# GpSimd's low parts of the mixer weights: a negated copy on ACT and an accumulating DMA in place of a subtraction

## The chip, the core and the metric

The kernel runs on one core of a Trainium2 chip (trn2). The core has five engines that work side by side, each through its own instructions in order: TensorE (PE, the matmuls; PEld are its weight loads), VectorE (DVE), ScalarE (ACT), GpSimd (POOL) and SyncE (SP, which issues most DMAs). ACT and POOL issue DMAs too. They wait for one another through semaphores. The metric is the time of one execution on the device in microseconds (us); lower is better.

## The reference

A bidirectional encoder of two layers over 512 tokens of 1024 channels, all in float32. A layer is a half-weighted SwiGLU block, a mixer, and another half-weighted SwiGLU block:

```python
for l in range(DEPTH):                       # DEPTH = 2
    x = x + 0.5 * swiglu(rmsnorm(x, ffn1_norm[l]), ...)      # 1024 -> 2816 -> 1024
    h = rmsnorm(x, mix_norm[l]); p = h @ w_in[l]             # 1024 -> 2048
    a, f, q, k, v = split(p)                                 # 256, 256, 512, 512, 512
    y_pool = pool_mixer(a, pool_w[l], pool_scale[l])         # window means minus token, a map, a scale
    y_four = fourier_mixer(f, fourier_w[l])                  # real part of a 2-D DFT, a map
    y_attn = diff_attention(q, k, v, lam, ...)               # 4 heads, softmax minus lam * softmax
    x = x + concat(y_pool, y_four, y_attn) @ w_out[l]        # 1024 -> 1024
    x = x + 0.5 * swiglu(rmsnorm(x, ffn2_norm[l]), ...)
return rmsnorm(x, final_norm)
```

## The kernel before

Channels lie on the 128 partitions and tokens along a row, so `x` is eight tiles of 128x512. TensorE multiplies in a faster float32 form that keeps fewer bits (`F32R`). To keep the accuracy, every operand is split into a high part `hi`, rounded to that form, and a low part `lo = x - hi`; a product is then three matmuls (`mm3`): high by high (L107), high by low (L108), low by high (L109).

**Weights.** They arrive in pieces of 128x1024 (512 KB), or 128x768, on SP's queue (L158), each in a staging tile `st`, of which there are seven. Some pieces of the SwiGLU blocks have a second piece added by an accumulating DMA that POOL issues (L160, L175), since these blocks use a scheme with fewer multiplications on sums of weights. `split` makes the operand of a piece: ACT copies `st` into `hi` (L103), then VectorE or GpSimd writes `lo = st - hi` (L104). There are four `hi` and four `lo` tiles, handed out in turn; a new one is written when the matmuls of the operand four places before it are done. `produce` runs three operands ahead of the matmuls (AHEAD), and loads five pieces ahead (RAWS).

**The mixer.** A mixer has twelve groups of weights of two pieces each, so 24 operands: P0 to P3 (queries and keys of a head), V0 and V1 (values), A (pooling group), F (Fourier group), and W0a, W1a, W2, W3 (the output projection). P1, P2, V1 and W3 stand in the table `ON_VECTOR`, and their low parts are written by VectorE. Those of the other eight, 16 operands in a mixer and 32 in all, are written by GpSimd.

The steps of a mixer are emitted in the order of the table `ORDER`, and a scheduler then places each engine's instructions. The steps that matter here, in that order: N is the norm of the mixer's input; P0 to P3 project; E0 to E3 split a head's queries and keys (`qs`, `kh`, `kl`: copies on ACT, differences on DVE); S is the scores of a head and a block of queries (DVE adds the bias and finds the maximum, ACT takes the exponential, one of three engines scales, DVE joins both softmaxes at L574, all in tiles `sc`); T transposes the scores on PE (`th`, `tl` are their parts); VE scales the values (`vh`, `vl`); X multiplies scores by values (`AV`, then `osq`, `osh`, `osl` for the head's norm); Y ends the head (`t`, `yo`, `yh`, `yl`); AE makes the window sums of the pooling group (`pad`, `win`, `m`), PL0 and PL1 multiply them by the pooling map (`PL`; the parts of `m` are tiles `g`); GH, FE, FG, FD are the Fourier group; W0a to W3 multiply by the output projection.

What sets an order there: each engine is in order, so a copy on ACT that waits holds up what stands behind it, and the same on POOL, whose queue also holds the sums of squares for the norms (L282), scalings of scores (L573), low parts of head outputs (`yl`, `osl`) and the issues of accumulating DMAs.

## Time and profile before

| | us |
|---|---|
| three runs | 1862.51, 1863.81, 1864.34 (median 1863.81) |
| profiled execution, its time | 1862.69 |
| profiled execution, its span | 1860.9 |
| mixer of the first layer, about | 374 to 565 |
| mixer of the second layer, about | 1285 to 1476 |
| POOL busy in the span | 307.2 |
| of it the 32 subtractions of weight pieces | 82.1 |

The span runs from the first instruction to the end of the last one of the profiled execution; 1.8 us of its time lie around it. A row of a timeline reads: start, length (both in us), engine, line of the kernel, operation, what it writes and reads, and in brackets how long the engine was idle before it and what ended that. "PE L109" is the matmul of line 109. Rows that group instructions give the busy time and the mean length in ns of one, and behind the bar the idle time of the engine ahead of them with what ended most of it. The lines that the argument needs are shown in the prediction.

### The profile page before, as it was taken

What the parts mean: (1) busy time and instruction counts of PE and PEld (TensorE: products, weight loads), DVE (VectorE), ACT (ScalarE), POOL (GpSimd) and SP (SyncE); (2) the same over time, 40 slices, a digit from 0 to 9 for tenths busy, and PEclk for the clock granted to TensorE, in tenths of its full rate; (3) what the DMA queues carried; (4) which work ended last, traced back from release to release, by engine and by line L of the source; (5) the groups of instructions that cost most, each with busy time, mean ns of one, the idle gap of its engine ahead of it and who ended that gap; (6) DMA issues with size and microseconds to landing.
All of it is one profiled execution on the core that took longest, in us unless ns stands there. A gap on an engine that the chain in (4) does not pass through costs nothing.

```text
span 1860.9 us, 28011 instructions
## 1 busy us (share of the span) xinstructions
PE 1773.0 (95%) x11249; PEld 1604.4 (86%) x11249; DVE 1355.0 (73%) x1962; ACT 853.6 (46%) x1193; POOL 307.2 (17%) x272
## 2 busy tenths in 40 slices
PE   7899999999798999999989999999987989999997
PEld 7889989877577989989889899898776888899896
DVE  6865856889779774856898477478978896568474
ACT  6433524457446433524554244243864554244243
POOL 1101101223313101101130010103232220010101
PEclk9899999999899999999999999999998999999998
DMA  8666857433215757857578586664221366586561
GB/s 250 146 168 150 199 131 170 136 94 91 71 35 125 175 154 158 202 139 164 155 156 205 125 204 159 141 167 137 69 80 49 83 149 181 128 186 181 130 165 46
DMA packets 76738, 262.91 MB, mean 141 GB/s; under 512 B 8640, under 2 KB 11712, under 8 KB 76608
## 3 DMA queue, kind: packets, MB, share of 16 engines
q0 software_dynamic: 24768, 90.19, 28.5%
q1 hardware_dynamic: 48672, 167.26, 27.7%
q10 hardware_dynamic: 3168, 3.68, 0.7%
q8 instruction: 88, 1.44, 0.3%
q14 instruction: 42, 0.34, 0.1%
HBM read 258.99 MB, written 2.10 MB: 140 GB/s over the span
## 4 chain that ended last, share of the span: by engine, by line
PE 78%; DVE 11%; ACT 4%; DMA 3%; issue 3%; POOL 0%; DVEq 0%; ACTq 0%; SPq 0%; POOLq 0%
PE dn L107 8%; PE dn L108 7%; PE dn L109 7%; PE qg L414 4%; PE qg L415 4%; PE qg L416 4%; PE qe L414 4%; PE qe L415 4%; PE qe L416 4%; PE qa L416 4%; PE qa L415 4%; PE qa L414 4%; DMA st<-in_gu 3%; DVE lo L104 2%; PE qb L415 2%
## 5 line engine op out<-in xcount | busy, mean ns | idle before, releaser
L103 ACT ACTIVATE hi<-st 128x1024 fp32r<-128x1024 f32 (+2 forms) x452 | 466.5, 1037 | 668.2 <-PE dn L108 216.7
L104 DVE TENSOR_TENSOR lo<-st,hi 128x1024 fp32r<-128x1024 f32 (+2 forms) x420 | 505.4, 1206 | 179.2 <-ACT hi L103 178.2
L108 PE MATMUL dn<-al,hi 128*128 128x512 f32 x704 | 274.6, 390 | 0.0
L109 PE MATMUL dn<-ah,lo 128*128 128x512 f32 x704 | 274.0, 389 | 0.0
L107 PE MATMUL dn<-ah,hi 128*128 128x512 f32 x704 | 271.9, 392 | 0.6
L175 POOL DMA_DIRECT2D st<-in_gu x129 | 116.0, 903 | 656.7 <-DVE lo L104 546.7
L414 PE MATMUL qg<-xh,hi 128*128 128x256 f32 x688 | 197.4, 287 | 9.0 <-DVE w L432 7.9
L415 PE MATMUL qg<-xh,lo 128*128 128x256 f32 x688 | 196.7, 286 | 0.0
L416 PE MATMUL qg<-xl,hi 128*128 128x256 f32 x688 | 196.7, 286 | 0.0
L414 PE MATMUL qe<-xh,hi 128*128 128x256 f32 x608 | 173.3, 285 | 14.6 <-ACT xh L103 8.4
L512 DVE SCALAR_TENSOR_TENSOR x<-dn,x 128x512 f32<-128x512 f32 x96 | 66.1, 688 | 164.7 <-PE dn L109 164.7
L415 PE MATMUL qe<-xh,lo 128*128 128x256 f32 x608 | 172.5, 284 | 2.1 <-DVE lo L104 2.1
L416 PE MATMUL qe<-xl,hi 128*128 128x256 f32 x608 | 172.4, 283 | 1.8 <-DVE xl L104 1.8
L107 PEld LDWEIGHTS dn<-ah,hi 128*128 128x128 f32 x704 | 131.3, 188 | 32.5 <-ACT ah L103 6.5
L108 PEld LDWEIGHTS dn<-al,hi 128*128 128x128 f32 x704 | 132.2, 188 | 28.9 <-DVE al L104 2.4
L109 PEld LDWEIGHTS dn<-ah,lo 128*128 128x128 f32 x704 | 132.2, 188 | 26.7
L414 PEld LDWEIGHTS qg<-xh,hi 128*128 128x128 f32 x688 | 134.1, 195 | 9.8 <-DVE w L432 8.3
L415 PEld LDWEIGHTS qg<-xh,lo 128*128 128x128 f32 x688 | 134.2, 195 | 0.0
L416 PEld LDWEIGHTS qg<-xl,hi 128*128 128x128 f32 x688 | 134.2, 195 | 0.0
L414 PEld LDWEIGHTS qe<-xh,hi 128*128 128x128 f32 x608 | 116.7, 192 | 17.9 <-ACT xh L103 9.2
L414 PE MATMUL qa<-xo,hi 128*128 128x256 f32 x424 | 120.9, 285 | 5.0 <-ACT q L423 5.0
L416 PE MATMUL qa<-xo,hi 128*128 128x256 f32 x424 | 121.3, 286 | 2.8 <-DVE xo L104 2.8
(268 smaller groups left out, 4138.0 us busy)
## 6 DMA issues: line engine op xcount, KB each, us to landing
st<-in_gu SPq DMA_DIRECT2D x176, 512.0 KB, 4.6
st<-in_gu POOLq DMA_DIRECT2D x172, 512.0 KB, 5.7
st<-in_dn SPq DMA_DIRECT2D x64, 512.0 KB, 3.9
st<-in_dn SPq DMA_DIRECT2D x32, 384.0 KB, 3.2
st<-in_qk SPq DMA_DIRECT2D x16, 512.0 KB, 3.6
st<-in_wo SPq DMA_DIRECT2D x16, 512.0 KB, 3.6
st<-in_wv SPq DMA_DIRECT2D x8, 512.0 KB, 3.9
st<-in_wfa SPq DMA_DIRECT2D x8, 512.0 KB, 3.8
```

The lines of the kernel that those rows point to most:

```text
L103: A.activation(hi, src, AF.Copy)
L104: (lo_eng or V).tensor_tensor(lo, src, f(hi), SUB)
L107: T.matmul(o, lh, rh, start=start, stop=False)
L108: T.matmul(o, lh, rl, start=False, stop=False)
L109: T.matmul(o, ll, rh, start=False, stop=stop)
L175: G.dma_start(t[:, 0:w], then, accum_op=ADD)
L414: T.matmul(o, wh[:, s], xh, start=start and p == 0 and z == 0, stop=False, **k)
L415: T.matmul(o, wl[:, s], xh, start=False, stop=False, **k)
L416: T.matmul(o, wh[:, s], xl, start=False, stop=stop and p == NK - 1 and z == 1, **k)
L512: V.scalar_tensor_tensor(X[m], b, 0.5, X[m], MUL, ADD)
```

## The change

For the eight weight groups that GpSimd served, the recipe now names no engine. `produce` handles such a piece in three steps: ACT copies `st` into `hi` as before; ACT copies `hi` into `lo` with a scale of -1; and POOL issues a DMA that adds the staged tile `st` to `lo`, from on-chip memory to on-chip memory, 512 KB. The low part is then `-hi + st`, the same difference. VectorE's pieces and all SwiGLU pieces are as before.

```diff
-                                operand_of(raw(src[x][:, z * 1024 : (z + 1) * 1024]), eng=V if x in ON_VECTOR else G)
+                                operand_of(raw(src[x][:, z * 1024 : (z + 1) * 1024]), eng=V if x in ON_VECTOR else None)
...
             for j in range(parts):
                 s = slice(j * q, (j + 1) * q)
-                split(t[:, s], hi[:, s], lo[:, s], eng)
+                if eng is not None:
+                    split(t[:, s], hi[:, s], lo[:, s], eng)
+                    continue
+
+                A.activation(hi[:, s], t[:, s], AF.Copy)
+                A.activation(lo[:, s], f(hi[:, s]), AF.Copy, scale=-1.0)
+                G.dma_start(lo[:, s], t[:, s], accum_op=ADD)
             if then is not None:
```

In the changed file the lines behind these are six higher: the high part is at L177, the negated copy at L178, the new DMA at L179, and for example L573 becomes L579.

The scheduler moves instructions around the new ones. Three places, all in the first mixer; the second has the same.

POOL at the start of the mixer, where the first two low parts (those of P0) stand among the sums of squares of the norm. Before:

```order
L282 TENSOR_TENSOR sq_3521<-sq_3521,sq_3586 128x512
L104 TENSOR_TENSOR lo_3658<-st_3523,hi_3657 128x1024
L282 TENSOR_TENSOR sq_3521<-sq_3521,sq_3619 128x512
L282 TENSOR_TENSOR sq_3521<-sq_3521,sq_3652 128x512
L104 TENSOR_TENSOR lo_3691<-st_3556,hi_3690 128x1024
```

And after:

```order
L288 TENSOR_TENSOR sq_3521<-sq_3521,sq_3586 128x512
L288 TENSOR_TENSOR sq_3521<-sq_3521,sq_3619 128x512
L179 DMA lo_3658<-st_3523 128x1024
L288 TENSOR_TENSOR sq_3521<-sq_3521,sq_3652 128x512
L179 DMA lo_3692<-st_3556 128x1024
```

Each low part is now a DMA issue, and stands one sum of squares later.

ACT at the step E1, behind the second high part of V0 (`hi`); `qs`, `kh` and `kl` are the parts of head 1's queries and keys. Before:

```order
L103 ACTIVATE hi_3935<-st_3755 128x1024
L540 ACTIVATE qs_3915<-tq_3911 64x512
L541 ACTIVATE kh_3916<-tk_3912 64x512
L544 ACTIVATE kh_3916<-tk_3912 64x512
L540 ACTIVATE qs_3924<-tq_3911 64x512
L545 ACTIVATE kl_3917<-kl_3917 64x512
L541 ACTIVATE kh_3925<-tk_3912 64x512
L544 ACTIVATE kh_3925<-tk_3912 64x512
L545 ACTIVATE kl_3926<-kl_3926 64x512
```

And after:

```order
L177 ACTIVATE hi_3938<-st_3757 128x1024
L546 ACTIVATE qs_3918<-tq_3914 64x512
L547 ACTIVATE kh_3919<-tk_3915 64x512
L550 ACTIVATE kh_3919<-tk_3915 64x512
L546 ACTIVATE qs_3927<-tq_3914 64x512
L551 ACTIVATE kl_3920<-kl_3920 64x512
L547 ACTIVATE kh_3928<-tk_3915 64x512
L550 ACTIVATE kh_3928<-tk_3915 64x512
L178 ACTIVATE lo_3939<-hi_3938 128x1024
L551 ACTIVATE kl_3929<-kl_3929 64x512
```

The negated copy stands between the last `kh` and the last `kl`.

ACT at the transposed scores of head 0 (`th`), a high part of the weights of group A, and the values `vh`. Before:

```order
L103 ACTIVATE th_4328<-T_409_4323 128x512
L103 ACTIVATE th_4337<-T_412_4332 128x512
L103 ACTIVATE th_4346<-T_415_4341 128x512
L103 ACTIVATE th_4355<-T_418_4350 128x512
L103 ACTIVATE hi_4578<-st_4109 128x1024
L713 DMA fw_4419<-in_fw 128x512
L714 DMA cs_4420<-in_dft_c 128x256
L644 ACTIVATE vh_4430<-v_4105,rcol_4428 128x512
```

And after:

```order
L103 ACTIVATE th_4333<-T_409_4328 128x512
L103 ACTIVATE th_4342<-T_412_4337 128x512
L103 ACTIVATE th_4351<-T_415_4346 128x512
L177 ACTIVATE hi_4585<-st_4113 128x1024
L103 ACTIVATE th_4360<-T_418_4355 128x512
L178 ACTIVATE lo_4586<-hi_4585 128x1024
L719 DMA fw_4426<-in_fw 128x512
L720 DMA cs_4427<-in_dft_c 128x256
L650 ACTIVATE vh_4437<-v_4109,rcol_4435 128x512
```

The high part moves ahead of the last `th`, and the negated copy stands ahead of the first `vh`.

## The prediction

> **What bounds the kernel now.** I read the page first: the busy shares, then the chain of work that ended last.

> ```profile
> span 1860.9 us, 28011 instructions
> PE 1773.0 (95%) x11249; PEld 1604.4 (86%) x11249; DVE 1355.0 (73%) x1962; ACT 853.6 (46%) x1193; POOL 307.2 (17%) x272
> PE 78%; DVE 11%; ACT 4%; DMA 3%; issue 3%; POOL 0%; DVEq 0%; ACTq 0%; SPq 0%; POOLq 0%
> ```

> TensorE is the bound, and POOL has no share of the chain. The change touches the two mixers alone, so next I cut the first mixer into stretches (columns: length; busy time and number of PE, weight loads, DVE, ACT, POOL; granted clock; DMA share; GB/s).

> ```profile
> 374.00:412.00 38.00, 36.76 (x160) 29.66 (x159) 32.31 (x50) 21.16 (x31) 8.87 (x4) 1.00 0.37 114
> 412.00:452.00 40.00, 38.27 (x182) 30.40 (x182) 38.68 (x106) 33.14 (x69) 12.83 (x7) 1.00 0.31 92
> 452.00:487.00 35.00, 31.39 (x140) 25.34 (x139) 26.45 (x47) 21.70 (x38) 14.86 (x10) 0.95 0.17 51
> 487.00:518.00 31.00, 20.89 (x88) 15.87 (x86) 24.02 (x64) 13.15 (x27) 7.58 (x4) 0.89 0.27 68
> 518.00:565.00 47.00, 46.60 (x230) 39.34 (x231) 38.63 (x72) 22.05 (x41) 5.88 (x3) 0.96 0.20 49
> ```

> PE is idle for 1.2, 1.7, 3.6, 10.1 and 0.4 us: 17 us of the mixer's 191 are all that can be won by waiting less. DVE is nearly full until 452 and ACT has 7 us left between 412 and 452, so both matter there. The single waits of PE show who ends them.

> ```profile
> 408.31 0.50 PE L557 MATMUL S<-kl,qs 128*128 128x512 f32 x1 [0.91 <-ACT kl L545]
> 441.53 1.09 PE L582 MATMUL T<-ident,sc 128*128 128x128 f32 x8 [1.10 <-DVE sc L574]
> 447.00 0.50 PE L107 MATMUL AV<-th,vh 128*128 128x512 f32 x1 [0.48 <-DVE vl L645]
> 470.55 0.79 PE L259 MATMUL ss<-osl,ones 128*128 128x512 f32 x1 [0.85 <-POOL osl L104]
> 501.99 0.50 PE L107 MATMUL PL<-g,g 128*128 128x512 f32 x1 [2.71 <-ACT g L103]
> 508.42 0.80 PE L108 MATMUL PL<-g,g 128*128 128x512 f32 x1 [5.46 <-DVE g L104]
> ```

> None of them waits for a low part `lo` of a weight. So the subtraction is not late for TensorE; if it costs anything, it is by what it does to DVE.

> **What goes, and what comes.** The rows grouped by form, and the DMA issues of the page:

> ```profile
> L104 POOL TENSOR_TENSOR lo<-st,hi 128x1024 fp32r<-128x1024 f32 x32 | 82.1, 2565 | 138.7 <-ACT hi L103 124.5 <-DVE lp L615 14.2
> L175 POOL DMA_DIRECT2D st<-in_gu x129 | 116.0, 903 | 656.7 <-DVE lo L104 546.7 <-PE wo L109 44.2 <-DMA st<-in_dn 21.8
> L103 ACT ACTIVATE hi<-st 128x1024 fp32r<-128x1024 f32 x416 | 438.3, 1058 | 618.7 <-PE dn L108 207.4 <-PE qg L416 94.5 <-issue 75.0
> st<-in_gu POOLq DMA_DIRECT2D x172, 512.0 KB, 5.7
> ```

> POOL loses 32 subtractions of 2.57 us (82 us) and gets 32 DMA issues of 0.90 (29 us). ACT gets 32 more copies of 128x1024; the row of such a copy says 1.06 us, 34 us in all, 17 in each mixer. Each `lo` lands about 5.7 us after its DMA is issued, instead of 2.6 us after POOL starts.

> **The gain: DVE stops standing behind POOL.** Beside three of POOL's subtractions stand these rows of DVE (timeline, two engines put together):

> ```profile
> 397.28 2.41 POOL L104 TENSOR_TENSOR lo<-st,hi 128x1024 fp32r<-128x1024 f32 x1 [2.32 <-ACT hi L103]
> 397.76 2.48 DVE L542 TENSOR_TENSOR qs<-tq,qs 64x512 fp32r<-64x512 f32 x1 [0.74 <-ACT qs L540]
> 400.98 0.69 DVE L542 TENSOR_TENSOR qs<-tq,qs 64x512 fp32r<-64x512 f32 x1
> ...
> 437.02 2.40 POOL L104 TENSOR_TENSOR lo<-st,hi 128x1024 fp32r<-128x1024 f32 x1 [0.21 <-ACT hi L103]
> 437.38 2.59 DVE L574 SCALAR_TENSOR_TENSOR sc<-sc,rc,sc 128x512 f32<-128x512 f32 x1
> 442.22 0.75 DVE L574 SCALAR_TENSOR_TENSOR sc<-sc,rc,sc 128x512 f32<-128x512 f32 x1
> ...
> 496.24 1.51 DVE L674 SCALAR_TENSOR_TENSOR m<-win,pad 64x512 f32<-64x512 f32 x1
> 500.30 0.70 DVE L669 TENSOR_TENSOR win<-pad 128x527 f32<-128x527 f32 x1
> 501.50 3.00 POOL L104 TENSOR_TENSOR lo<-st,hi 128x1024 fp32r<-128x1024 f32 x1 [4.29 <-ACT hi L103]
> 501.58 4.20 DVE L669 TENSOR_TENSOR win<-win 128x525 f32<-128x525 f32 x3
> ```

> The same operation takes 0.69 us when POOL is idle, and ends with POOL's instruction when that runs. The stalls are 1.8 us (`qs`), 1.8 (`sc`), 0.8 (`m`, as large as `qs`) and 2.1 (three `win` of 0.70 against 4.20). A DMA issue of POOL does no arithmetic on the tile, so I take them as gone. What reaches PE is less, because ACT's new copies stand in the same chains. I go from one wait of PE to the next, with these rows of ACT and one of DVE:

> ```profile
> 422.64 0.63 ACT L545 ACTIVATE kl<-kl 64x512 fp32r<-64x512 f32 x1 [2.15 <-DVE kl L543]
> 444.28 1.06 ACT L103 ACTIVATE hi<-st 128x1024 fp32r<-128x1024 f32 x1 [0.21 <-PE v L109]
> 460.16 2.10 DVE L251 TENSOR_TENSOR t<-t,v 128x512 f32<-128x512 f32 x1 [0.70 <-ACT t L242]
> 467.89 0.60 ACT L596 ACTIVATE osq<-AV 128x512 f32<-128x512 f32 x1 [0.40 <-POOL yl L104]
> 501.32 0.61 ACT L103 ACTIVATE g<-m 128x512 fp32r<-128x512 f32 x1
> ```

> 1. To 408: `qs` is 1.8 us shorter, and ACT waits less for `kl`; but the new copy for V0 stands in front of the last `kl` of E1 (order of ACT). ACT's four copies after `hi` end at 399.55; `kl` 0.63, two `kh` 1.28, the new copy 1.06 and the last `kl` 0.63 make 403.15, where it ends at 403.64 now: **-0.5 us** at PE.
> 2. To 447: ACT's idle 2.15 us ahead of `kl` at 422.64 hide one new copy, and a second takes back what that wins. The stall at 437.38 goes, so the transposes at 441.53 come 1.6 us sooner. But then ACT has three `th`, the `hi` that waits for PE's last `v` (444.28, then 442.7), the fourth `th`, a new copy, and only then `vh`: 442.7 + 1.06 + 0.6 + 1.05 = 445.4, where `vh` starts at 445.5 now. PE's `AV` is where it was, **-0.1**, and its wait grows from 0.5 to about 2 us.
> 3. To 470.6: a new copy stands ahead of the four `th` and of `osq`; its 0.4 us of waiting for POOL's `yl` hide part, as do the 1.4 us by which `t` at 460.16 gets shorter in this head's norm. In sum **+0.3**, so PE is at +0.2.
> 4. To 508.4: ACT's new copies push `g` (501.32) to about 502.7, so the wait that is 2.71 now becomes 3.5. The long one, 5.46, ends with DVE, which works without a pause from 496.2 to 508.4. It loses 0.8 + 2.1 us of stalls and gets about 0.4 us of new waits for ACT: **-2.4**.
> 5. After 518 PE is dense. The last two copies there cost nothing as long as PE has other matmuls in front (0.4 us idle in 47).

> That is 0.2 - 2.4 = -2.2 us for a mixer. The second mixer runs the same instructions, so I take it twice: **-4.4 us**. The new wait stands in POOL's queue: its DMA waits for ACT's second copy, and behind it stand `yl`, `osl` and the first accumulating loads of the next FFN. The copy follows `hi` by about 1 us and the issue takes 0.9, together less than the 2.57 us that these stood behind before.

> **The landing, which the trace doesn't have.** No transfer from SBUF to SBUF is in it. It takes at least POOL's issue, 0.9 us; the median accumulating transfer takes 5.7, and the chain shows one of 12.0 (596.57, below). I take 5.7, the same queue, size and addition. It is needed soonest for the first two operands, those of P0:

> ```profile
> 362.83 2.69 POOL L104 TENSOR_TENSOR lo<-st,hi 128x1024 fp32r<-128x1024 f32 x1 [1.50 <-ACT hi L103]
> 365.48 2.00 POOL L282 TENSOR_TENSOR sq<-sq,sq 128x512 f32<-128x512 f32 x1
> 371.06 2.58 POOL L104 TENSOR_TENSOR lo<-st,hi 128x1024 fp32r<-128x1024 f32 x1
> 374.36 0.39 PE L109 MATMUL pp<-xh,lo 128*128 128x512 f32 x1
> ...
> 596.57 11.98 DMA st<-in_gu
> ```

> In the new order that add of squares stands before the first DMA: it starts soon after 363, when its square is there, takes up to 2.0 us, so issue at about 365.3, landing 371.0, needed 374.4. The second: `hi` ready at about 370.3 (POOL's subtraction of 371.06 waited for an add of squares, not for it), copy done 371.3, landing 377.0, needed eight groups of three matmuls later, 374.4 + 8 x 0.68 = 379.8. So 2.8 us are to spare. At 12 us they would be late by 2.6 and 3.5. The next is V0, whose second operand has its copy by 402.5 and is needed after the scores of 408 to 412. The staged tile is free some 4 us later too; its next load is for an operand seven places on, and 24 operands in 191 us stand 8 us apart, so that costs nothing.

> **A rule weighed.** After waits PE runs slower for a while:

> ```profile
> 470.00:474.00 4.00, 3.45 (x9) 2.72 (x9) 3.11 (x4) 3.78 (x7) 0.50 (x1) 0.57 0.00 0
> 509.00:513.00 4.00, 4.00 (x14) 3.20 (x13) 1.45 (x2) 0.79 (x2) 0.00 (x0) 0.70 0.00 0
> ```

> The granted clock (the figure behind POOL's) drops to a mean of 0.57 after the wait of 0.85 at 470.55 and another just ahead of it, and to 0.70 after those of 2.71 and 5.46. Over 4 us that is 1.7 and 1.2 us of matmul time. [...]

> **The rivals.**
> - *ACT takes it all.* ACT has 6.9 us left between 412 and 452, and four copies take 4.2. If step 2 ends at +1 instead of -0.1, and steps 3 and 4 each lose another 0.5, the mixer is at -0.2. Time: 0 to -0.4 us, 1863.6. For it: the chain from 424 to 436 is ACT. Against it: step 4's long wait is DVE's.
> - *The low parts of P0 land late* (slower). It decides from 8.5 us of landing on; at 12 us PE waits 3.5 us in each mixer and then loses 1.7 by its clock as after 470: 2 x (5.2 - 2.2) = +6.0 us, 1869.8. For it: reading both operands in SBUF and writing another type is new. Against it: 5.7 is the median under load, too.
> - *The clock follows.* If the slow stretch after 508 goes in each mixer, 2 x 1.2 us come on top: 1857.0. If one comes at 447, it is the first rival.
> - *The stalls stay*, since POOL's issue blocks DVE as well: 0.9 us instead of 2.57 for each, so a third of the 2.9 us of step 4 comes back, 1.0 in a mixer: 1861.4. Nothing on the page shows DVE waiting for a DMA issue of POOL.

> **The numbers.** The profiled execution took 1862.7 us (span 1860.9 and 1.8 around it), 1.1 below the median 1863.8. So 1862.7 - 4.4 = 1858.3 for it, **1859.4** in medians, of which 1863.8 - 4.4 is the sum. About 0.2%, 3.7 us, is what a measurement of this kernel tells from no change: faster means below 1860.1. Chances: the forecast 0.48 (1857 to 1862; of it 0.33 faster, 0.15 same), ACT takes it 0.22 (0.20 same, 0.01 on each side), the stalls stay 0.05 (same), late landing 0.12 (0.11 slower, 0.01 same), the clock 0.13 (0.12 faster, 0.01 same). Faster 0.46, same 0.42, slower 0.12. The range leaves out the far end of the late landing and of the clock: 1854 to 1868.

> **What would show it.** Right: 32 ACT copies of about 1.05 us at line 178, DVE's `qs`, `sc` and `win` at 0.7 beside them, no wait of PE at the transposes, 2 us at `AV`, about 3 us instead of 5.46 at the second PL matmul. Wrong: a wait of PE on `lo` in P0; a DMA landing over 8 us; DVE rows of 1.5 us and more beside POOL's issues; or the 5.46 unchanged because DVE waits for ACT's `sc`.

## The result, and the profile after

After takes 1854.96 us (median of 6 runs, 1851.79 to 1858.33), and before, run beside it on the same chip, 1864.34 (6 runs). The ratio is 0.9945, with a 95% interval of 0.9933 to 0.9957: 9.4 us faster. The forecast was 4.4 us faster (1859.4, range 1854 to 1868). So the sign was right and the size about half. On a second chip the same two kernels gave 1855.53 and 1867.12, a ratio of 0.994 (0.9925 to 0.9956), 11.6 us. The profiled execution of after took 1856.4 us. The first lines of its page:

```profile
span 1854.4 us, 28082 instructions
PE 1767.0 (95%) x11249; PEld 1600.8 (86%) x11249; DVE 1314.8 (71%) x1962; ACT 884.8 (48%) x1225; POOL 250.0 (13%) x272
```

Span minus PE's busy time is 87.4 us, and before it was 1860.9 - 1773.0 = 87.9. So in these two executions PE waits equally long. What fell is its busy time, by 6.0 us, for the same 11249 matmuls. The same shows in the two mixers, cut from the first matmul of `pp` to the last of `wo` (columns: length; busy time and number of PE, weight loads, DVE, ACT, POOL; granted clock; DMA share; GB/s). Before:

```profile
373.91:576.15 202.24, 185.16 (x845) 149.93 (x844) 171.19 (x348) 120.00 (x218) 56.73 (x34) 0.97 0.29 77
1285.01:1487.45 202.44, 186.05 (x845) 150.38 (x844) 172.06 (x348) 120.01 (x218) 56.69 (x34) 0.96 0.28 77
```

and after:

```profile
374.76:573.62 198.86, 182.61 (x845) 148.43 (x844) 151.93 (x346) 132.73 (x231) 28.71 (x32) 0.98 0.48 118
1281.93:1481.16 199.23, 182.91 (x845) 148.68 (x844) 151.96 (x345) 132.76 (x231) 29.38 (x32) 0.98 0.48 118
```

A mixer is 3.4 and 3.2 us shorter. PE's idle time in it (length minus busy) went from 17.1 and 16.4 to 16.3 and 16.3 us; its busy time fell by 2.6 and 3.1. DVE's busy time fell by 19 and 20 us, and ACT's grew by 13 in each.

What was added costs what the forecast said: a copy 1.06 us, an issue 0.89, a landing 5.2 (rows by form, and the page's DMA issues). No matmul waits for such a `lo`.

```profile
L178 ACT ACTIVATE lo<-hi 128x1024 fp32r<-128x1024 f32 x32 | 33.8, 1055 | 0.6
L179 POOL DMA_DIRECT2D lo<-st x32 | 28.5, 890 | 167.2 <-ACT lo L178 129.8 <-DVE tk L541 17.6 <-PE T L588 10.5
lo<-st POOLq DMA_DIRECT2D x32, 512.0 KB, 5.2
```

DVE's stalls are gone too (timeline of DVE): `qs` 0.69 instead of 2.48, `sc` 0.74 instead of 2.59, and the three `win` behind the first 1.44 and 0.68 us instead of 4.20.

```profile
398.56 0.69 DVE L548 TENSOR_TENSOR qs<-tq,qs 64x512 fp32r<-64x512 f32 x1 [0.69 <-ACT qs L546]
499.61 0.71 DVE L675 TENSOR_TENSOR win<-pad 128x527 f32<-128x527 f32 x1
500.24 0.74 DVE L580 SCALAR_TENSOR_TENSOR sc<-sc,rc,sc 128x512 f32<-128x512 f32 x1
501.64 1.44 DVE L675 TENSOR_TENSOR win<-win 128x525 f32<-128x525 f32 x2
503.66 0.68 DVE L675 TENSOR_TENSOR win<-win 128x512 f32<-128x512 f32 x1
```

PE's waits in the first mixer, with the row of ACT that explains the new one at 453.47:

```profile
408.70 0.49 PE L563 MATMUL S<-kl,qs 128*128 128x512 f32 x1 [0.46 <-ACT kl L551]
445.50 0.55 PE L588 MATMUL T<-ident,sc 128*128 128x128 f32 x3 [0.61 <-DVE tl L104]
447.08 0.50 PE L107 MATMUL AV<-th,vh 128*128 128x512 f32 x1 [0.93 <-DVE vl L651]
450.20 2.07 ACT L103 ACTIVATE th<-T 128x512 fp32r<-128x512 f32 x4 [2.23 <-PE AV L109]
453.47 0.50 PE L264 MATMUL ss<-osh,ones 128*128 128x512 f32 x1 [1.16 <-ACT osh L103]
472.49 0.50 PE L265 MATMUL ss<-osl,ones 128*128 128x512 f32 x1 [0.85 <-POOL osl L104]
485.87 0.39 PE L107 MATMUL GH<-g,g 128*128 128x256 f32 x1 [1.98 <-ACT g L103]
503.51 0.50 PE L107 MATMUL PL<-g,g 128*128 128x512 f32 x1 [3.04 <-ACT g L103]
506.98 0.80 PE L108 MATMUL PL<-g,g 128*128 128x512 f32 x1 [2.51 <-DVE g L104]
```

The long wait of 5.46 is 2.51. But 1.16 us are new at 453: counted from the first `pp` of the mixer (374.76 us here, 373.91 in before), ACT's four `th` come 1.6 us later than in before (450.20 against 447.80 on the two clocks). The wait at GH grew from 1.23 to 1.98.

**The granted clock.** Here it is cut into pieces of 3.41 us around the PL waits. Before:

```profile
497.70:501.11 3.41, 1.57 (x7) 0.96 (x6) 3.30 (x16) 2.79 (x5) 0.00 (x0) 1.00 0.51 154
501.11:504.53 3.42, 0.97 (x3) 0.48 (x3) 3.39 (x3) 0.83 (x2) 3.00 (x1) 1.00 0.00 0
504.53:507.95 3.42, 0.00 (x0) 0.00 (x0) 3.26 (x9) 0.00 (x0) 0.00 (x0) 0.50 0.52 153
507.95:511.36 3.41, 2.94 (x7) 2.36 (x8) 1.55 (x5) 0.63 (x1) 0.00 (x0) 0.50 0.00 0
511.36:514.77 3.41, 3.25 (x14) 2.34 (x13) 1.94 (x7) 1.29 (x3) 0.60 (x1) 1.00 0.00 0
514.77:518.19 3.42, 1.46 (x7) 0.93 (x7) 3.32 (x12) 3.39 (x9) 0.68 (x1) 1.00 0.00 0
518.19:521.60 3.41, 3.20 (x12) 2.82 (x13) 3.41 (x9) 1.35 (x2) 0.00 (x0) 0.50 0.00 0
```

and after:

```profile
501.44:504.85 3.41, 0.96 (x3) 0.49 (x3) 3.38 (x8) 2.02 (x3) 0.85 (x1) 1.00 1.06 209
504.85:508.26 3.41, 1.28 (x3) 1.10 (x4) 2.12 (x10) 0.00 (x0) 0.00 (x0) 0.50 1.01 220
508.26:511.68 3.42, 3.42 (x9) 2.68 (x9) 1.42 (x2) 0.63 (x1) 0.00 (x0) 0.50 0.71 230
511.68:515.09 3.41, 2.31 (x10) 1.56 (x9) 2.42 (x9) 2.24 (x5) 1.27 (x1) 1.00 0.00 0
515.09:518.50 3.41, 2.19 (x10) 1.48 (x11) 3.31 (x12) 3.09 (x9) 0.00 (x0) 1.00 0.00 0
```

In these rows a piece has one clock, 1.00 or 0.50 (full and half rate: in before, matmuls of 128x512 stand 0.23 us apart from 511.49 to 514.23 and 0.43 apart from 509.01 to 511.15). A piece at full rate in which PE was busy for 0.96, 0.97 or 1.46 of 3.41 us is followed by one at 0.50; one with 1.57, 2.19 or 2.31 is not. Cut on from 370 to 1840 us at edges 3.413 us apart, these two profiles have no piece at any other clock: 13 of before's 431 pieces are at 0.50, and 8 of after's (the edges lie at other times in after than in before). In the two, all twelve pieces at full rate with 1.46 us of PE or less are followed by half rate, and none with 1.57 or more is; two profiles do not make a rule of it. The waits at 516 and 518 (1.48 and 0.84 us) are the same in both kernels. In before they fell into one piece, and the next ran at half rate; in after they fell into two, and it didn't. The stretch that the prediction showed at 470 is gone in the same way: the two waits there are 1.53 and 0.85 us in before and 1.55 and 0.85 in after. In before they left one piece with 1.19 us of PE:

```profile
466.98:470.39 3.41, 1.19 (x5) 0.41 (x3) 3.31 (x6) 2.96 (x7) 2.04 (x2) 1.00 0.49 154
```

In after an edge parts them, and the clock stays at 1.00, though PE idles for 2 us of the 4 behind 470:

```profile
467.31:470.72 3.41, 2.27 (x11) 1.53 (x9) 2.77 (x6) 3.23 (x8) 1.38 (x2) 1.00 0.78 234
470.00:474.00 4.00, 2.01 (x8) 1.44 (x9) 3.62 (x7) 3.59 (x7) 1.27 (x1) 1.00 0.68 144
```

The second mixer has the same: before runs at half rate in one piece from 1381.8 us, three from 1412.5 and one from 1429.6; after only in two from 1412.8.

### The profile page after: what moved, and what is told of

It is laid out like the page before. It is cut to its first block, busy times and chain, and to the rows that moved or that the text cites. A ratio compares the mean times of both kernels' runs of the same rounds, so it can differ in the third digit from the quotient of the medians.

```text
span 1854.4 us, 28082 instructions
## 1 busy us (share of the span) xinstructions
PE 1767.0 (95%) x11249; PEld 1600.8 (86%) x11249; DVE 1314.8 (71%) x1962; ACT 884.8 (48%) x1225; POOL 250.0 (13%) x272
## 3 DMA queue, kind: packets, MB, share of 16 engines
q8 instruction: 88, 1.44, 0.3%
## 4 chain that ended last, share of the span: by engine, by line
PE 77%; DVE 8%; ACT 6%; DMA 5%; issue 2%; POOL 0%; SPq 0%; ACTq 0%; DVEq 0%; POOLq 0%
PE dn L107 8%; PE dn L108 7%; PE dn L109 7%; PE qg L420 4%; DMA st<-in_gu 4%; PE qg L421 4%; PE qg L422 4%; PE qe L420 4%; PE qe L421 4%; PE qe L422 4%; PE qa L422 4%; PE qa L421 4%; PE qa L420 4%; DVE lo L104 2%; PE qb L421 2%
## 5 line engine op out<-in xcount | busy, mean ns | idle before, releaser
L103 ACT ACTIVATE hi<-st 128x1024 fp32r<-128x1024 f32 (+2 forms) x420 | 433.1, 1036 | 645.7 <-PE dn L108 218.1
L104 DVE TENSOR_TENSOR lo<-st,hi 128x1024 fp32r<-128x1024 f32 (+2 forms) x420 | 503.5, 1202 | 182.9 <-ACT hi L103 179.8
L108 PE MATMUL dn<-al,hi 128*128 128x512 f32 x704 | 274.6, 390 | 0.0
L109 PE MATMUL dn<-ah,lo 128*128 128x512 f32 x704 | 274.1, 389 | 0.0
L107 PE MATMUL dn<-ah,hi 128*128 128x512 f32 x704 | 272.0, 392 | 0.6
L107 PEld LDWEIGHTS dn<-ah,hi 128*128 128x128 f32 x704 | 131.3, 188 | 32.5 <-ACT ah L103 6.5
L108 PEld LDWEIGHTS dn<-al,hi 128*128 128x128 f32 x704 | 132.2, 188 | 28.7 <-DVE al L104 2.4
L109 PEld LDWEIGHTS dn<-ah,lo 128*128 128x128 f32 x704 | 132.2, 188 | 26.7
## 6 DMA issues: line engine op xcount, KB each, us to landing
st<-in_gu SPq DMA_DIRECT2D x176, 512.0 KB, 4.5
st<-in_gu POOLq DMA_DIRECT2D x172, 512.0 KB, 5.6
st<-in_dn SPq DMA_DIRECT2D x64, 512.0 KB, 3.9
lo<-st POOLq DMA_DIRECT2D x32, 512.0 KB, 5.2
st<-in_qk SPq DMA_DIRECT2D x16, 512.0 KB, 3.7
st<-in_wo SPq DMA_DIRECT2D x16, 512.0 KB, 3.7
st<-in_wv SPq DMA_DIRECT2D x8, 512.0 KB, 4.4
```

Source lines behind the costliest of these rows:

```text
L103: A.activation(hi, src, AF.Copy)
L104: (lo_eng or V).tensor_tensor(lo, src, f(hi), SUB)
L107: T.matmul(o, lh, rh, start=start, stop=False)
L108: T.matmul(o, lh, rl, start=False, stop=False)
L109: T.matmul(o, ll, rh, start=False, stop=stop)
```

## The experiments

Two questions were open: which of the removed stalls gives the time, and how much of it is waiting and how much is clock. In the expectations, theory S says that the gain comes from VectorE's stalls behind GpSimd's two-operand arithmetic, Q that it comes from GpSimd's queue being free sooner, and C that a good part is granted clock. S4 is S narrowed to step 4 of the prediction, the wait at PL. Each group ran beside before on its own chip: medians of 1867.34 (23 runs), 1867.12 (14) and 1867.81 us (17). The clock in the table is the mean of the clocks of all runs of the kernel.

| kernel | median us | against before | 95% interval | clock |
|---|---|---|---|---|
| before (3 groups and before_again, 66 runs) | 1867.1 | | | 0.9793 |
| after_again | 1855.5 | 0.9940 | 0.9925 to 0.9956 | 0.9817 |
| act_only | 1873.1 | 1.0032 | 1.0022 to 1.0042 | 0.9782 |
| pool_tt | 1879.0 | 1.0059 | 1.0045 to 1.0073 | 0.9765 |
| pool_ts | 1883.5 | 1.0091 | 1.0076 to 1.0106 | 0.9765 |
| pool_hi | 1859.3 | 0.9962 | 0.9950 to 0.9974 | 0.9818 |
| w1a_only | 1859.3 | 0.9955 | 0.9942 to 0.9968 | 0.9805 |
| no_w1a | 1868.6 | 1.0007 | 0.9996 to 1.0017 | 0.9784 |
| w0a_w1a | 1856.7 | 0.9951 | 0.9933 to 0.9969 | 0.9813 |
| fill_before | 1862.7 | 0.9974 | 0.9965 to 0.9984 | 0.9841 |
| fill_after | 1853.9 | 0.9930 | 0.9917 to 0.9944 | 0.9843 |
| ord_x2 | 1853.6 | 0.9927 | 0.9911 to 0.9942 | 0.9812 |

**before_again**: before, unchanged.

> The kernel before, unchanged, for its granted clock in every run. After's six runs have a mean clock of 0.9835. Theory C (most of the gain is granted clock: PE's idle time fell by only 0.6 us in the two profiles, but its busy time by 6.0 for the same matmuls): mean clock here 0.979 to 0.981, time 1864. Rival S alone (the gain is idle time of PE): the clocks agree within 0.001, and the profile shows 4 us or more of PE idle time beyond after's.

Its 12 runs took 1866.97 us (median) with a mean clock of 0.980, as C expected. PE's idle time in the profile is 1861.8 - 1773.1 = 88.7 us against 87.4 in after, not the 4 us more that S alone asked for; but after_again, below, shows that this sum over the whole span is no safe measure. The profile has something else, too. A stall of W0a's subtraction that the prediction's profile did not show sits on DVE's `y` (2.76 us, elsewhere 0.69) and makes PE wait 3.83 instead of 1.23 us at GH:

```profile
477.66 2.61 POOL L104 TENSOR_TENSOR lo<-st,hi 128x1024 fp32r<-128x1024 f32 x1 [8.08 <-ACT hi L103]
478.06 2.76 DVE L253 SCALAR_TENSOR_TENSOR y<-t,y 128x512 f32<-128x512 f32 x1
484.90 0.58 PE L107 MATMUL GH<-g,g 128*128 128x256 f32 x1 [3.83 <-ACT g L103]
```

**act_only**: ACT's copy alone.

```diff
                 A.activation(hi[:, s], t[:, s], AF.Copy)
                 A.activation(lo[:, s], f(hi[:, s]), AF.Copy, scale=-1.0)
-                G.dma_start(lo[:, s], t[:, s], accum_op=ADD)
+                G.tensor_tensor(lo[:, s], t[:, s], f(hi[:, s]), SUB)
```

> ACT writes the negated high part as in after, but GpSimd then subtracts over it as before: the stalls of VectorE stay and ACT's 34 us are paid. Theory S (the gain comes from VectorE's stalls, ACT's copies cost something): 1866 to 1870, slower than before. Rival (ACT's copies are free): 1864, as before. If this is faster than before, the gain has nothing to do with GpSimd's arithmetic.

The copies with the stalls left in cost 5.8 us, more than S expected: they are not free. The price includes that each subtraction starts a copy later. The first PL wait is 4.43 us (2.71 in before), the second 4.77 (5.46).

**pool_tt** and **pool_ts**: GpSimd does useless work ahead of each DMA.

```diff
+                # pool_tt
+                for c, e in ((0, 384), (384, 768), (768, 1024)):
+                    G.tensor_tensor(dump[:, 0 : e - c], t[:, c:e], f(hi[:, c:e]), SUB)
+                # pool_ts
+                for c, e in ((0, 384), (384, 768), (640, 1024), (0, 384), (384, 768)):
+                    G.tensor_scalar(dump[:, 0 : e - c], t[:, c:e], 1.0, 1.0, MUL, MUL)
                 G.dma_start(lo[:, s], t[:, s], accum_op=ADD)
```

> After, with GpSimd still doing a subtraction of the same 128x1024 (in three pieces, bf16, into a tile that nobody reads) ahead of each of the 32 accumulating DMAs. Theory S (two-operand arithmetic of GpSimd stalls VectorE): the gain is gone, 1864 to 1870. Theory Q (the gain is that GpSimd's queue is free sooner): the same. If it stays at 1855, neither is the source.

> After, with GpSimd busy for about the same 2.6 us ahead of each of the 32 DMAs, but with operations of one tensor operand (5 of 128x384, bf16 out), beside which VectorE's rows were not longer (the eight 128x512 scalings of sc: 0.5 us of excess in 26 overlaps). Theory S: the gain stays, 1855 to 1857. Theory Q: it is gone, 1862 or more.

pool_tt lost the gain and more. For pool_ts, S expected 1855 to 1857 and Q 1862 or more; it took 1883.5. But it does not decide for Q, since it held the queue far longer than before does. One operand takes 3.84 us and an issue, 4.7 together against 2.57, and the `osl` that PE wants stands behind it:

```profile
477.66 3.84 POOL L180 TENSOR_SCALAR dump<-st 128x384 bf16<-128x384 f32 x5 [2.49 <-DMA st<-in_wo]
481.47 1.26 POOL L104 TENSOR_TENSOR osl<-osq,osh 128x512 fp32r<-128x512 f32 x1
482.78 0.79 PE L268 MATMUL ss<-osl,ones 128*128 128x512 f32 x1 [4.91 <-POOL osl L104]
```

**pool_hi** repeats it at the right size: two pieces that read `hi`, 1.3 us, and then the issue.

```diff
+                for c in (0, 384):
+                    G.tensor_scalar(dump, f(hi[:, c : c + 384]), 1.0, 1.0, MUL, MUL)
                 G.dma_start(lo[:, s], t[:, s], accum_op=ADD)
```

> After, with GpSimd held about 1.35 us (two one-operand operations of 128x384 that read the high part) ahead of each DMA's issue of 0.9, so about 2.25 us an operand, near the 2.57 of before, but with little stall of VectorE. Theory S: 6 us or more below before, the loss against after being the later landing. Theory Q (what counts is how long GpSimd's queue is held; 0.9 us gave -9 and 4.3 us in pool_ts gave +16): within 3 us of before.

It is 7.8 us below before in the medians (7.1 by the ratio), as S expected. So most of the gain stays while GpSimd is held for about 2.2 us an operand, near before's 2.57: at this length the queue is not what counts. DVE's busy time for the same 1962 instructions tells the three apart (pages of pool_tt, pool_ts and pool_hi; after has 1314.8, before 1355.0):

```profile
PE 1778.9 (95%) x11249; PEld 1607.4 (86%) x11249; DVE 1348.7 (72%) x1962; ACT 886.0 (47%) x1225; POOL 350.8 (19%) x368
PE 1775.5 (94%) x11249; PEld 1604.3 (85%) x11249; DVE 1324.6 (70%) x1962; ACT 885.0 (47%) x1225; POOL 356.3 (19%) x432
PE 1771.4 (95%) x11249; PEld 1604.1 (86%) x11249; DVE 1322.1 (71%) x1962; ACT 885.0 (48%) x1225; POOL 293.8 (16%) x336
```

Here two-operand work of GpSimd (104.4 us of it in pool_tt) costs DVE 34 us against after, one-operand work of about the same length (108.1 us in pool_ts) 10.

**after_again**: after beside before, for its clock.

> The kernel after, unchanged, beside before on the same chip, for more runs of its granted clock. Theory C (a good part of the gain is granted clock): mean clock 0.983 to 0.984 against before's 0.979 in 35 runs, ratio 0.993 to 0.996. If the clock was luck of six runs, it is 0.980 here and the ratio 0.996 to 0.998.

The ratio held, 0.9940. The clock of these six runs is 0.9817, between the two cases; all twelve of after have 0.9826, and the 66 of before 0.9793.

Its profile has a span of 1851.5 us and 1769.8 of PE: an idle time of 81.7 us, 5.7 less than the first profile of after. Splitting the four profiles at the ends of the mixers shows where that comes from:

| profile | both mixers, us | PE busy in them | PE idle in them | rest of the span |
|---|---|---|---|---|
| before | 404.7 | 371.2 | 33.5 | 1456.2 |
| before_again | 408.3 | 370.3 | 38.0 | 1453.5 |
| after | 398.1 | 365.5 | 32.6 | 1456.3 |
| after_again | 397.9 | 365.2 | 32.7 | 1453.6 |

The rest of the span varies by 2.8 us with or without the change; the difference between the kernels lies in the mixers, 6.6 us in the first pair and 10.4 in the second. Of it 5.7 and 5.0 us are PE's busy time, and 0.9 and 5.3 are waiting. In the first pair the busy time is clock: in pieces of the mixers at half rate PE is busy for 20.9 us in before's profile and for 10.2 in after's, and half of the difference is 5.3. In the second pair the granted clock of the two mixers is 0.97 and 0.97 in before_again and 0.98 and 0.98 in after_again.

**w1a_only** and **no_w1a**: the change for W1a alone, and for the other seven weight groups alone.

```diff
-    operand_of(raw(...), eng=V if x in ON_VECTOR else None)
+    operand_of(raw(...), eng=V if x in ON_VECTOR else None if x == "W1a" else G)    # w1a_only
+    operand_of(raw(...), eng=V if x in ON_VECTOR else G if x == "W1a" else None)    # no_w1a
```

> Before, with the new path for one operand of the eight, W1a, whose subtractions stand ahead of PE's longest wait (5.46 us, PL). Theory S4 (the gain is that wait, the other seven operands give nothing or cost): the wait falls to 2.5 to 3 us, the new waits at ss<-osh and GH that after shows do not come, and the time is at or below after's: 8 to 12 us below before. Rival (the stalls ahead of the scores and of the transposes matter too): 3 to 6 us below before, half of after's gain.

> The other half of w1a_only: seven operands by the new path, W1a by GpSimd's subtraction as before. w1a_only gave -7.8 us and the whole change -11.6. If the two parts add up: -4 us, and PE's wait of 5.46 us ahead of the second PL matmul is back. If the seven only cost ACT time (theory S4): 0 to +2 us. If clock and waits do not add up, it lies outside of -6 to +2.

W1a alone gives 7.8 us, just short of S4's 8 to 12 and more than its rival's 3 to 6; the other seven groups give nothing (0.8 slower, interval across 1). The PL waits follow, w1a_only first and no_w1a behind it:

```profile
502.23 0.80 PE L107 MATMUL PL<-g,g 128*128 128x512 f32 x1 [3.04 <-ACT g L103]
505.69 0.79 PE L108 MATMUL PL<-g,g 128*128 128x512 f32 x1 [1.82 <-DVE g L104]
```

```profile
505.46 0.80 PE L107 MATMUL PL<-g,g 128*128 128x512 f32 x1 [4.78 <-ACT g L103]
511.88 0.80 PE L108 MATMUL PL<-g,g 128*128 128x512 f32 x1 [4.77 <-DVE g L104]
```

With W1a alone PE waits 4.9 us there instead of 8.2, and the new waits at `ss<-osh` and GH do not come. In this profile the two mixers take 400.2 us, with PE idle for 27.4 and busy for 372.8: against the table above, what W1a gives here is waiting, and no clock comes with it. With the other seven groups PE waits 9.6: their copies on ACT bring `g` later, and W1a's subtraction still stalls DVE, which is busy for 1325.0 us, 10 more than in after. The two parts sum to 7.0 us, and the whole is 11.6 on this chip and 9.4 on the first. The gap of 4.6 or 2.4 us is about as large as the three intervals leave room for, so that the parts do not add up is not shown.

**w0a_w1a**: the same for W0a and W1a, after the stall that before_again showed.

> New path for W0a and W1a. The profile of before_again showed one stall that the profile of before did not: VectorE's y (L253) 2.76 us beside W0a's subtraction, and PE's wait at GH 3.83 instead of 1.23 us. If such stalls are part of what typical runs of before pay: 1 to 4 us faster than w1a_only, so -9 to -12. If it is a rare event, or ACT's copies in front of g take it back (1.98 us at GH in after): -7 to -8.

11.1 us below its before, 3.3 more than w1a_only, as expected if such stalls are common. But the two intervals overlap, so W0a's share is not settled. That the stall is not rare shows elsewhere: fill_before, which keeps W0a's subtraction, has it in its profile too, with 3.87 us of PE's waiting at GH in the first mixer.

**fill_before** and **fill_after**: matmuls of a zero tile in the PL wait, 20 of them in before and 10 in after. They add zeros to the bank.

```diff
-                mm3(o, pwh[:, s], pwl[:, s], mh, ml, True, True)
+                T.matmul(o, pwh[:, s], mh, start=True, stop=False)
+                if i == 0:
+                    for _ in range(20):
+                        T.matmul(o, zero, mh, start=False, stop=False)
+                T.matmul(o, pwh[:, s], ml, start=False, stop=False)
+                T.matmul(o, pwl[:, s], mh, start=False, stop=True)
```

> Before, with 20 matmuls of a zero tile (128x512, added to the PL bank) between the first and the second PL matmul, where PE waits 5.46 us for VectorE; they add nothing to the result and end no wait sooner. Theory C (an idle wait costs PE half of its rate in the next 3.4 us): no half-rate stretch at 504 and 518, mean clock 0.982 or more, 3 to 6 us below before. Rival (only the length of the waits counts): 0 to 2 us above before.

> After, with 10 matmuls of a zero tile (about 2.2 us) between the first and the second PL matmul, where PE waits 2.51 us. Theory C: mean clock up by 0.001 to 0.003 against after's 0.982, 2 to 4 us faster than after (-13 to -16). Rival (after's wait is too short to cost clock): within 1 us of after.

fill_before is 4.5 us faster than before (0.9965 to 0.9984), though the wait that is filled did not get shorter: the second PL matmul stands 6.48 us behind the first, in before 6.43. From the first to the second, and the 3.41 us behind the second, in before and then in fill_before:

```profile
501.99:508.42 6.43, 0.97 (x3) 0.49 (x4) 6.24 (x12) 0.00 (x0) 2.51 (x1) 0.70 0.28 82
508.42:511.83 3.41, 3.41 (x9) 2.75 (x10) 1.54 (x4) 0.63 (x1) 0.00 (x0) 0.57 0.00 0
```

```profile
503.59:510.07 6.48, 5.05 (x21) 3.87 (x21) 6.29 (x12) 0.00 (x0) 2.56 (x1) 1.00 0.27 81
510.07:513.48 3.41, 3.41 (x15) 2.83 (x16) 1.55 (x4) 0.63 (x1) 0.00 (x0) 1.00 0.00 0
```

PE gets through 15 matmuls there instead of 9. C holds, by the time and the mean clock; the half-rate stretch at 518, which it expected to go too, stays in the first mixer of this profile (`wo` matmuls of 128x512 stand 0.43 us apart from 519.72 to 520.58, and 0.23 from 522.55 on); the second mixer as a whole has a clock of 0.99, in before 0.96. The profiled run itself took 1864.33 us, more than the kernel's median of 1862.65, with the wait at GH named above in it. In fill_after the clock rises to 0.9843 and the time falls to 1853.9, some 2 us below after; the intervals overlap, so it doesn't decide between C and its rival.

**ord_x2**: w0a_w1a with one entry moved in the order of the mixer.

```diff
-    "... AE0 AE1 F PL0 X2 S31 S33 PL1 ..."
+    "... AE0 AE1 F X2 PL0 S31 S33 PL1 ..."
```

> w0a_w1a with X2 (the product AV of head 2, 12 matmuls that were ready) placed ahead of PL0 in the order, so that some 10 matmuls of 0.22 us stand in front of the wait at PL instead of behind it. If PE's wait there is worth its length and the clock behind it: 2.2 us a mixer and 0 to 1.5 of clock, so 4 to 7 us faster than w0a_w1a. If VectorE sets the end of this stage anyway: no change.

3.1 us below w0a_w1a, less than expected, and the intervals overlap. The ready `AV` matmuls shorten the waits at the first PL pair to 1.87 and 1.48, but the next PL then waits 2.75 us where it waited 1.46 (and 0.84 behind it). Of all kernels here this one and fill_after have the lowest medians, 14 us below before; that they beat after is not shown.

```profile
503.08 0.50 PE L107 MATMUL PL<-g,g 128*128 128x512 f32 x1 [1.87 <-ACT g L103]
506.12 0.80 PE L108 MATMUL PL<-g,g 128*128 128x512 f32 x1 [1.48 <-DVE g L104]
512.22 0.80 PE L107 MATMUL PL<-g,g 128*128 128x512 f32 x1 [2.75 <-ACT g L103]
```

## Why the prediction was right in kind and short in size

Its sum can be checked at its own waits. This is where PE stands in the first mixer, counted from the mixer's first `pp`, after minus before:

| at | before | after | difference | forecast |
|---|---|---|---|---|
| S, step 1 | 34.40 | 33.94 | -0.5 | -0.5 |
| AV, step 2 | 73.09 | 72.32 | -0.8 | -0.1 |
| ss<-osl, step 3 | 96.64 | 97.73 | +1.1 | +0.2 |
| second PL, step 4 | 134.51 | 132.22 | -2.3 | -2.2 |
| end | 202.24 | 198.86 | -3.4 | -2.2 |

- **Steps 1 and 5** came out: the wait at S is 0.46, and the last copies cost nothing. The landing, taken as 5.7, was 5.2.
- **Step 2** came out better. `vh` starts 70.8 us behind the first `pp`, where the forecast had 71.5 and before 71.6, and PE waits 0.61 us at the transposes and 0.93 at `AV`, not 0 and 2.
- **Step 3** was too cheap: +1.9 us instead of +0.3, which leaves PE at +1.1 and not at +0.2. The forecast let the four `th` behind `vh` start on time. ACT gets to them 1.6 us late, after a wait of 2.23 us for the last `AV` matmul that before doesn't have, and that is PE's new 1.16 at 453.
- **Step 4** was right at PL: the two waits went from 2.71 and 5.46 to 3.04 and 2.51, against 3.5 and about 3 forecast (in the second mixer the long one went from 4.79 to 2.51). It left out the copies ahead of `g` at GH, 0.75 us. w1a_only and no_w1a show that W1a's stalls, ahead of PL, carry most of the gain and that the other seven groups give nothing by themselves.
- **The clock was the term that was mis-sized.** It stood in the sum at nothing, and the prediction gave a slow stretch less in each mixer a chance of 0.13 as a rival. In the first mixer the stretch at 470 went between steps 3 and 4 and the one at 518 behind step 4; the idle time fell by only 0.8 us and 2.6 came from PE's busy time. Without what the stretch at 470 gave back, half of a piece of 3.4 us, PE would have stood at about -0.6 at the second PL matmul and not at -2.3: that the position there meets the forecast is luck, since the errors in step 3 and at GH and the error in the clock hid each other. That the stretch at 470 is gone is not to be put down to shorter waits: the two there are 1.53 and 0.85 us in before and 1.55 and 0.85 in after, and only in before did one piece hold both. No run shows that the sum could do without a clock term: in before, a piece of 3.41 us with 1.96 of idle (514.77 to 518.19, busy 1.46) was followed by one at 0.50, and the mean clock of all runs rose from 0.9793 in before to 0.9826 in after.

The forecast's 4.4 us were all waiting. In the profiled pair the PL waits give 2.6 us in the first mixer and 2.0 in the second, the other waits of the mixers take 3.7 of that back, and 5.7 of the mixers' 6.6 us are PE's busy time. So the PL waits went about as forecast, and the time of this pair came mostly from a term that the sum didn't have.

How much is clock over all runs? The mean clock rose from 0.9793 to 0.9826, by 0.0033 of 1860 us: 6.1 us if PE was busy through all of it. fill_before gained 4.5 us for a rise of 0.0048, that is 8.9 by the same sum, so about half of it counted there. As an estimate, then, 3 to 6 of the 9.4 to 11.6 us are clock; the two pairs of profiles say 5.0 and 5.7. The rest is waiting, and how much of it there is depends on the execution: 0.9 us in the first pair and 5.3 in the second, where before_again has the stall at GH that W0a's subtraction makes. before's profiled executions are on the fast side of their own runs: 1862.7 us where the median is 1864.3, and 1863.5 us (clock 0.981) where it is 1867.0 (0.980). So a common run of before loses 1.6 to 3.4 us that the profiled one doesn't. What else makes up these, and whether the whole change gives more than its parts, stays open.

Of the rivals, the clock follows came true beside the forecast, not in its place; its slow stretch behind 508 went at 518. ACT takes it all was right that the copies are not free: act_only is 5.8 us slower, and the first PL wait is 4.43 us there and 4.78 in no_w1a, where W1a's subtraction still runs. In after it is 3.04, and the shorter second wait pays for that. Late landing did not come: the two transfers of P0 landed 5.3 and 5.4 us after their issue, the longest of the 32 took 8.5, and `lo` was never waited for. (Two sums of the rivals are slightly off: at 12 us of landing the first operand of P0 would be late by 2.9 us, not 2.6, and the mixer of ACT takes it all ends at -0.1, not -0.2.) The stalls stay is refuted by the DVE rows.

## What to carry to other kernels

Here work of GpSimd on two tensors cost the time of VectorE beside it rather than its own (`qs` 2.48 us instead of 0.69; DVE 34 us busier in pool_tt than in after): look for rows of VectorE that end with GpSimd's, and move first the one that stands ahead of the bound engine's longest wait; here one weight group of eight gave 7.8 of 11.6 us. A wait of TensorE cost its length here and at places half of the clock behind it (0.50 for 3.41 us from 518.19 in before), and 20 empty matmuls in the wait at PL gave 4.5 us in fill_before, so putting ready matmuls, or even empty ones, into a wait is worth trying. And look at more than one profile of the kernel before: a stall may be missing from the one you read, as the one at GH was here (PE waits 1.23 us in before, 3.83 in before_again).
